# A hybrid recurrence and feed-forward layer: activations turned in 32x32 blocks by VectorE and placed by DRAM transfers, with silu(z) multiplied in the output stage

## The chip, the cores and the metric

The kernel runs on one core of a Trainium2 chip. The metric is the device time of one execution in microseconds, here the median of three runs. Inputs and outputs lie in DRAM; five engines (PE for matmuls, DVE, ACT, POOL, and SP, which only issues transfers) run their own instruction streams and wait for each other through semaphores.

## The reference, cut to what matters

One layer is computed for 2048 rows of one new stream and for 8 running streams of 16 rows, 17 tiles of 128 rows in all. Everything is float32.

```
h   = RMSNorm_pre(x);  P = h @ w_in -> q, k, v, z (512 each), b, a (4), B, C, H (512 each)
q, k, v: causal conv(4), SiLU, q and k L2-normalised; gated delta rule over chunks -> o (4 heads x 128)
o   = RMSNorm_head(o; gdn_norm_w) * silu(z)
y   = B * causal_conv3(C * H)
x   = x + RMSNorm_post(concat(o, y) @ w_o)
h   = RMSNorm_pre2(x)                       # norm_ffn_pre
x   = x + RMSNorm_post2((silu(h @ w_gate) * (h @ w_up)) @ w_down)
```

D_MODEL is 1024, D_FF 2816. The states and the last rows before the convolutions are outputs too.

## The kernel before, in words

Each float32 operand of a large matmul is split into a high and a low part, and a product is three matmuls (high x high, high x low, low x high), accumulated in PSUM. Rows of a tile lie on the 128 partitions or, turned, features lie on them; a matmul contracts over the partitions, so an activation has to be turned so that its features are there.

The program has four stages. (1) 0 to 860 us: the in-projection and the recurrence, in five groups of tiles (`GROUPS = [[0..3], [4..7], [8, 9, 10], [11, 12, 16], [13, 14, 15]]`; tile 16 is the sample rows). PE's order here is written out by hand: actions of the recurrence are put at slots between the in-projection's matmuls. `out_norm` scales a tile's output o (rows on partitions, 4 heads x 128 features) by its norm; `out_turn` (L717) turns the four 128x128 blocks on PE (L720) into a PSUM bank, multiplies on DVE by the gain `g_hd` and by silu(z) (L722), which already lies with features on partitions, and stores the tile `ot` to the DRAM tensor `mixo[t]` on ACT's queue. The other half of the mixture goes to `mixs` per group. (2) 860 to about 1065 us: the output stage. `o_load(t)` loads `mr` from `mixo[t]` (L1095, 128 rows of 2 KB) and `mixs` (L1097) and the residual row tile `xo` (L1099), all on SP's queue. `o_tile(t)` splits `mr` into `mh` and `ml` (L1068 on ACT, L1069 on DVE), runs 48 matmuls of 512 columns against the split `w_o` (L1116, into `dbank` and `tbank`), squares the sums (L1120, ACT), takes the root on POOL (`rstd`, L147), multiplies by `gpost` (L1125, DVE) and adds the residual (L1126). `o_rows(t)` makes the feed-forward input: squares (L1135, ACT), root (L147, POOL), `hx` = row scaled (L1139, DVE), eight PE transposes into two PSUM banks `ftbank` (L1145), two DVE multiplications by the gain `g_ffn` into `ht` (L1146), and a store of `ht` to `hTd` on ACT's queue (L1149). There is one `mr` buffer and three `mh`/`ml` pairs of half a tile. While tiles 7 to 13 are in this stage the first feed-forward group is prepared: `ffn_load` (L1236) loads `fh` from `hTd` for the six tiles of the group, one load of 128 rows of 3 KB for each of the 8 blocks of 128 features, and `ffn_prep` forms sums and splits of them. (3) 1090 to 1985 us: gate and up products (L1351) for the groups of tiles 0 to 5, 6 to 11 and 12 to 16, in a Strassen-like form; the weights are combined and split on ACT, DVE and POOL (L1326, L1327), stored once to `fsplit` and loaded again for later groups. The `fh` of groups 1 and 2 are loaded in this stage (L1236, 8 loads each). (4) to 2457 us: the down product (L1528) and the final norm.

Apart from PE's hand-written slots in stage 1, each engine's order and the order of SP's queue are set when the program is built, by a scheduler that simulates it with its own costs. On the chip each queue then runs in exactly that order: SP issues transfers one after the other, and an instruction whose wait is not fulfilled holds up all behind it on its engine.

## Time and profile before

| | before |
|---|---|
| runs (us) | 2456.3, 2461.07, 2460.23; median 2460.23 |
| profiled execution: span, first to last instruction (us) | 2457.2 |
| time of the profiled execution outside its span | not given separately; the three runs lie 0.9 below to 3.9 above its span |
| PE busy | 2428.1 us, 99% |
| DVE, ACT, POOL busy | 1619.9, 1045.7, 578.6 us |
| DMA, mean rate | 228 GB/s |

PE is busy nearly throughout, so its idle time and its instructions make up the span. A matmul is pipelined: its listed duration runs past the start of the next one, and what an instruction costs PE is read from the distance between starts.

### The profile page before, as it was taken

How to read it: one execution, taken by the hardware profiler on the slowest of the kernel's cores; microseconds unless marked ns; L12 is line 12 of the kernel's file. 1: busy time of each engine (PE TensorE's matmuls, PEld its weight loads, DVE VectorE, ACT ScalarE, POOL GpSimd, SP SyncE). 2: the span in 40 equal slices, each digit the busy share in tenths (PEclk: the TensorE clock that was granted, in tenths of full speed). 3: DMA queues.
4: the chain of work that ended last, by engine and by line, in shares of the span. 5: the costliest groups of instructions: out<-in, count | busy, mean ns of one | idle time of the engine just before them, and what ended most of it. 6: DMA issues, size and time to landing. Idle time of an engine off the chain costs nothing.

```text
span 2457.2 us, 39354 instructions
## 1 busy us (share of the span) xinstructions
PE 2428.1 (99%) x14376; PEld 2222.2 (90%) x14376; DVE 1619.9 (66%) x3079; ACT 1045.7 (43%) x2338; POOL 578.6 (24%) x664
## 2 busy tenths in 40 slices
PE   9999999999999999999999999999999999999997
PEld 7888889999989978899999999999999988887886
DVE  7875755746667366788888644556555565677698
ACT  6545546546444343444444422324333345333343
POOL 1101001001110000156655200000000046455563
PEclk9999999999999999999999999999999999999999
DMA  7774655666776466598877788778898743333465
GB/s 272 262 246 163 220 194 203 244 222 232 273 261 234 162 222 225 195 336 301 289 268 259 266 261 266 252 246 273 307 298 283 249 144 118 116 111 122 132 224 191
DMA packets 263465, 561.38 MB, mean 228 GB/s; under 512 B 25188, under 2 KB 144680, under 8 KB 245992
## 3 DMA queue, kind: packets, MB, share of 16 engines
q1 hardware_dynamic: 146864, 486.98, 57.3%
q10 hardware_dynamic: 116184, 70.85, 9.5%
q8 instruction: 113, 1.85, 0.3%
q0 software_dynamic: 224, 1.05, 0.1%
q14 instruction: 80, 0.66, 0.1%
HBM read 400.09 MB, written 158.70 MB: 227 GB/s over the span
## 4 chain that ended last, share of the span: by engine, by line
PE 87%; DVE 6%; DMA 2%; issue 2%; POOL 2%; ACT 1%; SPq 0%; DVEq 0%; ACTq 0%; POOLq 0%
PE fbank L1351 36%; PE dbank L317 26%; PE fbank L1528 11%; PE dbank L1116 4%; PE tbank L1116 4%; POOL dw L1201 1%; DVE xr L1551 1%; PE tbank L375 1%; DVE acc L1488 1%; PE gbank L592 1%; PE gbank L599 1%; PE obank L769 1%; POOL as L1511 1%; PE obank L747 1%; PE gbank L739 1%
## 5 line engine op out<-in xcount | busy, mean ns | idle before, releaser
L1351 PE MATMUL fbank<-xh,fw 128*128 128x384 f32 (+1 forms) x3696 | 898.1, 326 | 2.7 <-ACT m L1385 2.5
L317 PE MATMUL dbank<-hi,w 128*128 128x384 f32 (+1 forms) x2240 | 655.6, 363 | 2.2 <-DMA w<-wsplit 1.4
L1351 PEld LDWEIGHTS fbank<-xh,fw 128*128 128x128 f32 x3696 | 651.6, 188 | 3.4 <-ACT m L1385 2.8
L1351 PE MATMUL fbank<-xl,fw 128*128 128x384 f32 (+1 forms) x1848 | 602.4, 326 | 0.0
L317 PEld LDWEIGHTS dbank<-hi,w 128*128 128x128 f32 x2240 | 412.6, 188 | 43.9 <-issue 4.0
L1528 PE MATMUL fbank<-dw,as 128*128 128x512 f32 x1782 | 420.2, 392 | 3.4 <-DVE as L1511 1.2
L1528 PEld LDWEIGHTS fbank<-dw,as 128*128 128x128 f32 x1782 | 332.9, 188 | 82.1 <-POOL as L1511 3.5
L317 PE MATMUL dbank<-lo,w 128*128 128x384 f32 (+1 forms) x1120 | 399.6, 357 | 0.3 <-DVE lo L232 0.3
L1351 PEld LDWEIGHTS fbank<-xl,fw 128*128 128x128 f32 x1848 | 347.3, 188 | 0.0
L317 PEld LDWEIGHTS dbank<-lo,w 128*128 128x128 f32 x1120 | 210.7, 188 | 16.6 <-DVE lo L232 0.6
L1511 POOL TENSOR_TENSOR as<-ar,as 128x256 fp32r<-128x256 f32 (+1 forms) x202 | 184.2, 924 | 171.1 <-ACT as L1508 168.7
L1488 DVE TENSOR_TENSOR acc<-acc,fbank 128x512 f32<-128x512 f32 x248 | 164.9, 681 | 90.2 <-PE fbank L1528 77.1
L1201 POOL TENSOR_TENSOR dw<-dr,dw 128x512 fp32r<-128x512 f32 x48 | 70.3, 1477 | 497.5 <-ACT dw L1199 497.3
L1508 ACT CAST as<-ar 128x256 fp32r<-128x256 f32 (+1 forms) x287 | 116.4, 427 | 166.8 <-PE fbank L1528 124.3
L1326 ACT CAST fw<-rg 128x512 fp32r<-128x512 f32 x124 | 77.2, 622 | 228.6 <-PE fbank L1351 138.3
L321 DVE SCALAR_TENSOR_TENSOR acc<-R,vec,acc 128x512 f32<-128x512 f32 (+2 forms) x180 | 120.9, 672 | 27.0 <-ACT acc L358 20.8
L1399 DVE TENSOR_TENSOR c<-u,fbank 128x384 f32<-128x384 f32 (+1 forms) x66 | 34.8, 528 | 95.5 <-PE fbank L1351 95.5
L1395 DVE TENSOR_TENSOR m<-m,m 128x384 f32<-128x384 f32 (+1 forms) x44 | 23.1, 525 | 82.8 <-ACT m L1385 82.8
L1327 POOL TENSOR_TENSOR fw<-rg,fw 128x512 fp32r<-128x512 f32 x44 | 65.3, 1485 | 45.9 <-ACT fw L1326 41.9
L1397 ACT ACTIVATE m<-fbank 128x384 f32<-128x384 f32 (+1 forms) x66 | 31.2, 473 | 96.4 <-PE fbank L1351 79.0
L350 POOL COPY hist<-R 128x3 f32<-128x3 f32 x60 | 20.1, 335 | 220.6 <-ACT R L326 171.5
L1402 ACT ACTIVATE c<-c 128x384 f32<-128x384 f32 (+1 forms) x66 | 33.4, 507 | 83.4 <-DVE c L1401 83.4
(395 smaller groups left out, 3575.6 us busy)
## 6 DMA issues: line engine op xcount, KB each, us to landing
w<-wsplit SPq DMA_DIRECT2D x105, 1024.0 KB, 4.9
fw<-fsplit SPq DMA_DIRECT2D x188, 512.0 KB, 4.8
fsplit<-fw SPq DMA_DIRECT2D x94, 512.0 KB, 3.6
partd<-pt ACTq DMA_DIRECT2D x86, 384.0 KB, 6.1
rg<-in_w_gu SPq DMA_DIRECT2D x62, 512.0 KB, 4.0
wsplit<-w SPq DMA_DIRECT2D x28, 1024.0 KB, 4.9
wr<-in_w_in SPq DMA_DIRECT2D x34, 512.0 KB, 5.8
ar<-partd SPq DMA_DIRECT2D x43, 384.0 KB, 3.1
```

The lines of the kernel that those rows point to most:

```text
L317: T.matmul(ps[:, :c], l[:, k, :], r[k][:, :c], start=(k == 0 and r is hi and l is wh), stop=(k == KD - 1 and l is wl))
L321: r = V.scalar_tensor_tensor(acc, raw(d), w[:, d:d + 1], acc, op0=ALU.mult, op1=ALU.add)
L1116: T.matmul(pss[n], m_[:, j, :], w_[k][:, n * 512:(n + 1) * 512], start=(k == 0 and ci == 0), stop=(k == KD - 1 and ci == 2))
L1201: e.tensor_tensor(out=w[1], in0=v, in1=w[0].bitcast(F32), op=ALU.subtract)
L1326: A.copy(w[:, 0], v)
L1327: e.tensor_tensor(out=w[:, 1], in0=v, in1=w[:, 0].bitcast(F32), op=ALU.subtract)
L1351: T.matmul(ps, w_[:, c], b_[k][:, :hw], start=(first and k == 0 and ci == 0), stop=(k == KH - 1 and ci == 2), skip_group_check=not first)
L1399: V.tensor_add(c21, u2, b3)
L1488: return eng.tensor_tensor(out=dst, in0=dst, in1=ps, op=ALU.add)
L1508: ins = A.copy(a[:, 0, :n], v)
L1511: e.tensor_tensor(out=a[:, 1, :n], in0=v, in1=a[:, 0, :n].bitcast(F32), op=ALU.subtract)
L1528: T.matmul(ps, a[:, x_, q * P:(q + 1) * P], w[y_], start=(start and q == 0 and ci == 0), stop=(q == c - 1 and ci == 2), skip_group_check=True)
```

## The change: turning moved to VectorE and to transfers

Both places that turned activations on PE now turn them on DVE in 32x32 blocks (an instruction that exchanges rows and columns inside each 32x32 block of a tile), and the blocks get to their places by the way in which the tile is stored to DRAM and loaded again.

- Recurrence output: `out_turn` is one DVE instruction, `V.transpose(ot, o)`. `mixo[t]` is now [4 heads, 4, 32*128], written in rows of 512 B (512 of them), and read by `o_load` in rows of 128 B (2048 of them). Features within a head come out in the order `turn` (a 4x32 index array turned), which the host applies to z's columns of `w_in`, to `gdn_norm_w` and to the first four blocks of rows of `w_o`.
- silu(z) and the gain: silu(z) of a group is stored to a new DRAM tensor `szd[gi]` on ACT's queue when its fourth head is done; `o_load` loads the tile's part `zr` (512 rows of 512 B) on SP's queue, and POOL multiplies the tile's `mr` by it, 128x512 (for tile 0, in `ahead`, eight loads and four POOL multiplications of 128x128). The gain `g_hd` goes into the split of `w_o`: for its first four blocks the ACT copy has a scale and the DVE subtraction becomes a scalar_tensor_tensor.
- Feed-forward rows: in `o_rows` the scaling and the gain are one DVE instruction for each half of 512 features, into a PSUM tile now called `hx`, followed by one DVE 32x32 transpose of the half into `ht`. The gain is a broadcast row tile `gffn` (128x1024), loaded on SP's queue behind `gpost`. `ht` is stored with 1024 rows of 512 B as before. `fh` is loaded in 3072 rows of 128 B (2560 in the group of five tiles) in place of 128 rows of 3 KB (2.5 KB). The features within a block of 128 come out in the order `turn`, which the host applies to the rows of the gate and up weights.

The diff, cut to its core (indices into the small vector table shift and are left out):

```
-    mixo = [dram.tile([P, H, P], F32, name=f"mixo{t}") for t in range(NT)]
+    mixo = [dram.tile([H, 4, 32 * P], F32, name=f"mixo{t}") for t in range(NT)]
+    szd = [dram.tile([P, H, len(g) * P], F32, name=f"szd{gi}") for gi, g in enumerate(GROUPS)]
...
-    hTd = [dram.tile([P, KD, len(g) * P], F32, name=f"hTd{gi}") for gi, g in enumerate(FGROUPS)]
+    hTd = [dram.tile([KD, 4 * len(g), 32 * P], F32, name=f"hTd{gi}") for gi, g in enumerate(FGROUPS)]
...
                 flush(mark["A"])
+                if h == 3:
+                    nc.scalar.dma_start(out=szd[g["gi"]], in_=g["sz"][:, :, :c])
...
         def out_turn(g, i, o):
-            ps = tbank()
-            for h in range(H):
-                T.transpose(ps[:, h * P:(h + 1) * P], o[:, h, :], ident)
             ot = wk.tile([P, H, P], F32, tag="ot", name="ot")
-            V.scalar_tensor_tensor(ot, h4(ps), g_hd, g["sz"][:, :, i * P:(i + 1) * P], op0=ALU.mult, op1=ALU.mult)
+            V.transpose(ot, o)
+            out = mixo[g["tiles"][i]].rearrange("h a (d x) -> (a d) h x", d=32)
             if i + 1 < g["npr"] or g["gi"] + 1 < len(GROUPS):
-                nc.scalar.dma_start(out=mixo[g["tiles"][i]], in_=ot)
+                nc.scalar.dma_start(out=out, in_=ot)
             else:
-                last_stores.append((mixo[g["tiles"][i]], ot))
+                last_stores.append((out, ot))
...
-            nc.sync.dma_start(out=vt, in_=mixo[0])
             gi, i = PLACE[0]
+            zs = [q[:, W1 - P:] for q in g["qT"]]
+            for h in range(H):
+                nc.sync.dma_start(out=vt[:, h].rearrange("p (a t) -> p a t", a=4), in_=mixo[0][h].rearrange("a (p t) -> p a t", t=32))
+                nc.sync.dma_start(out=zs[h], in_=szd[gi][:, h, i * P:(i + 1) * P])
             nc.sync.dma_start(out=sz, in_=mixs[gi][:, :, i * P:(i + 1) * P])
+            for h in range(H):
+                G.tensor_tensor(out=vt[:, h], in0=vt[:, h], in1=zs[h], op=ALU.mult)
...
+        def wo_split(k, a, b, v):
+            if k < H:
+                A.activation(a, v, AF.Copy, scale=g_hd)
+                V.scalar_tensor_tensor(b, v, g_hd, a.bitcast(F32), op0=ALU.mult, op1=ALU.subtract)
+            else:
+                A.copy(a, v)
+                V.tensor_sub(b, v, a.bitcast(F32))
...
         nc.sync.dma_start(out=gpost, in_=rows_[0].partition_broadcast(P))
+        nc.sync.dma_start(out=gffn, in_=rows_[2].partition_broadcast(P))
...
-                m = oa.tile([P, KD, P], F32, tag="mr", name="mr") if t > 1 else spare[2]
+                m = oa.tile([P, KD, P], F32, tag="mr", name="mr") if t > 1 else spare[1]
                 mr = m[:, 0:4], m[:, 4:8]
-                nc.sync.dma_start(out=mr[0], in_=mixo[t])
                 gi, i = PLACE[t]
+                zr = oa.tile([P, 4, P], F32, tag="zr", name="zr")
+                nc.sync.dma_start(out=mr[0].rearrange("p h (a t) -> p (h a) t", a=4), in_=mixo[t].rearrange("h a (p t) -> p (h a) t", t=32))
+                nc.sync.dma_start(out=zr, in_=szd[gi][:, :, i * P:(i + 1) * P])
                 nc.sync.dma_start(out=mr[1], in_=mixs[gi][:, :, i * P:(i + 1) * P])
+                G.tensor_tensor(out=mr[0], in0=mr[0], in1=zr, op=ALU.mult)
...
-            hx = op.tile([P, D], F32, tag="hx", name="hx") if t else spare[0]
-            V.tensor_scalar_mul(hx, xt, r)
-            ht = op.tile([P, KD, P], F32, tag="ht", name="ht") if t else spare[1]
+            ht = op.tile([P, D], F32, tag="ht", name="ht") if t else spare[0]
             for n in range(2):
-                ps = pft.tile([P, 512], F32, tag="t", name="ftbank")
-                for q in range(4):
-                    k = 4 * n + q
-                    T.transpose(ps[:, q * P:(q + 1) * P], hx[:, k * P:(k + 1) * P], ident)
-                V.tensor_mul(ht[:, 4 * n:4 * n + 4, :], ps.rearrange("p (k c) -> p k c", k=4),
-                             g_ffn[:, 4 * n:4 * n + 4].unsqueeze(2).broadcast_to([P, 4, P]))
+                c = slice(n * 512, (n + 1) * 512)
+                hx = pft.tile([P, 512], F32, tag="t", name="hx")
+                V.scalar_tensor_tensor(hx, xt[:, c], r, gffn[:, c], op0=ALU.mult, op1=ALU.mult)
+                V.transpose(ht[:, c], hx)
             gi, i = FPLACE[t]
-            nc.scalar.dma_start(out=hTd[gi][:, :, i * P:(i + 1) * P], in_=ht)
+            nc.scalar.dma_start(out=hTd[gi][:, 4 * i:4 * i + 4].rearrange("k a (d x) -> (a d) k x", d=32),
+                                in_=ht.rearrange("p (k x) -> p k x", k=KD))
...
-                nc.sync.dma_start(out=h[:, :2 * hw], in_=hTd[gi][:, k, :])
+                nc.sync.dma_start(out=h[:, :2 * hw].rearrange("p (m t) -> p m t", t=32), in_=hTd[gi][k].rearrange("m (p t) -> p m t", t=32))
...
+    turn = np.arange(P).reshape(4, 32).T.reshape(P)
...
+    cols = lambda c, b: off[c] + P * b + (turn if c == "z" else np.arange(P))
...
+    a["w_o"] = np.concatenate([w_o[:H, turn], w_o[H:]])
+    a["w_gu"] = gu.reshape(2, KD, P, NF, P)[:, :, turn].transpose(3, 0, 2, 1, 4)
```

The scheduler gives a new order. On SP's queue, at the place in the output stage where the first feed-forward group's `fh` is loaded, `mr_10257` is tile 9's mixture before and `mr_10155` with `zr_10156` after (the tile is the number behind `mixo`); `xo` are residual rows. Before:

```order
L1095 DMA mr_10257<-mixo9_69 128x512
L1097 DMA mr_10257<-mixs2_79 128x4x128
L1236 DMA fh_10118<-hTd0_110 128x768
L1236 DMA fh_10120<-hTd0_110 128x768
L1236 DMA fh_10122<-hTd0_110 128x768
L1236 DMA fh_10124<-hTd0_110 128x768
L1099 DMA xo_10137<-in_x 128x1024
L1236 DMA fh_10225<-hTd0_110 128x768
L1236 DMA fh_10227<-hTd0_110 128x768
L1236 DMA fh_10229<-hTd0_110 128x768
L1236 DMA fh_10231<-hTd0_110 128x768
L1095 DMA mr_10380<-mixo10_70 128x512
```

After, on the same queue at the same place:

```order
L1109 DMA zr_10156<-szd2_79 128x4x128
L1113 DMA xo_9929<-in_x 128x1024
L1247 DMA fh_10021<-hTd0_115 128x24x32
L1247 DMA fh_10023<-hTd0_115 128x24x32
L1247 DMA fh_10025<-hTd0_115 128x24x32
L1247 DMA fh_10027<-hTd0_115 128x24x32
L1247 DMA fh_10123<-hTd0_115 128x24x32
L1247 DMA fh_10125<-hTd0_115 128x24x32
L1247 DMA fh_10127<-hTd0_115 128x24x32
L1247 DMA fh_10129<-hTd0_115 128x24x32
L1108 DMA mr_10155<-mixo9_69 128x16x32
L1110 DMA mr_10155<-mixs2_84 128x4x128
```

Tile 9's mixture stood ahead of the eight `fh` loads and now stands behind all of them; its `zr` is still ahead. On POOL's queue, in the output stage, the rows are the two roots of each tile (`oxr` for the first norm, `oyr` for the second; `oxr_10219` is tile 8's) and, after the change, the multiplications by silu(z) (`mr_10037` is tile 8's mixture, `mr_10155` tile 9's, `mr_10273` tile 10's). After:

```order
L1111 TENSOR_TENSOR mr_10037<-mr_10037,zr_10038 128x512
L147 TENSOR_TENSOR oxr_9987<-oxm_9985,neghalf_181 128x1
L147 TENSOR_TENSOR oyr_9999<-oym_9997,neghalf_181 128x1
L147 TENSOR_TENSOR oxr_10101<-oxm_10099,neghalf_181 128x1
L147 TENSOR_TENSOR oyr_10113<-oym_10111,neghalf_181 128x1
L147 TENSOR_TENSOR oxr_10219<-oxm_10217,neghalf_181 128x1
L1111 TENSOR_TENSOR mr_10155<-mr_10155,zr_10156 128x512
L147 TENSOR_TENSOR oyr_10231<-oym_10229,neghalf_181 128x1
L1111 TENSOR_TENSOR mr_10273<-mr_10273,zr_10274 128x512
```

Before, only the alternating `oxr` and `oyr` rows stood there; now tile 9's multiplication stands behind `oxr_10219`, and each root behind a multiplication waits for that tile's loads.

## Rows read from the trace of the kernel before

**Rows 1.** The page: busy time of each engine, and the chain that ended last.
```profile
PE 2428.1 (99%) x14376; PEld 2222.2 (90%) x14376; DVE 1619.9 (66%) x3079; ACT 1045.7 (43%) x2338; POOL 578.6 (24%) x664
...
PE 87%; DVE 6%; DMA 2%; issue 2%; POOL 2%; ACT 1%; SPq 0%; DVEq 0%; ACTq 0%; POOLq 0%
```

**Rows 2.** Waits of PE: releaser, us in total, times, longest.
```profile
PE fbank L1351 <- ACT m L1385: 2.5, 1, 2.5
```

**Rows 3.** Groups of PE instructions: count, busy us, mean ns, idle before.
```profile
L1145 PE MATMUL ftbank<-cst,hx 128*128 128x128 f32 x136 | 17.7, 273 | 0.2 <-DVE hx L1139 0.2
L720 PE MATMUL tbank<-cst,o 128*128 128x128 f32 x64 | 9.7, 274 | 0.0
```

**Rows 4.** Timeline of PE around eight transposes: start, duration, instruction.
```profile
946.91 0.40 PE L1116 MATMUL tbank<-wol,mh 128*128 128x512 f32 x1
947.14 1.04 PE L1145 MATMUL ftbank<-cst,hx 128*128 128x128 f32 x8
947.93 0.47 PE L1116 MATMUL dbank<-woh,ml 128*128 128x512 f32 x1
948.25 0.39 PE L1116 MATMUL tbank<-woh,ml 128*128 128x512 f32 x1
```

**Rows 5.** Timeline of PE at tile 1's second half.
```profile
869.36 0.50 PE L1116 MATMUL dbank<-woh,mh 128*128 128x512 f32 x1 [0.49 <-ACT mh L1068]
```

**Rows 6.** Timeline of ACT and its queue in the output stage.
```profile
868.69 0.62 ACT L1068 CAST mh<-mr 128x512 fp32r<-128x512 f32 x1 [3.84 <-DMA mr<-mixo]
...
933.54 0.59 ACT L1120 ACTIVATE ojunk<-dbank 128x512 bf16<-128x512 f32 x1
...
950.89 0.52 ACTq L1149 DMA_DIRECT2D hTd<-ht  x1
...
957.47 0.62 ACT L1068 CAST mh<-mr 128x512 fp32r<-128x512 f32 x1 [3.97 <-DMA mr<-mixo]
```

**Rows 7.** Timeline of POOL after tile 5's matmuls.
```profile
935.47 0.55 POOL L147 TENSOR_TENSOR oxr<-oxm,neghalf 128x1 f32<-128x1 f32 x1 [5.03 <-DVE oxm L145]
```

**Rows 8.** Timeline of SP's queue at tile 9's loads.
```profile
952.87 0.33 SPq L1095 DMA_DIRECT2D mr<-mixo  x1
...
954.41 2.34 SPq L1236 DMA_DIRECT2D fh<-hTd  x4
...
957.27 2.29 SPq L1236 DMA_DIRECT2D fh<-hTd  x4
```

**Rows 9.** Transfers at 857.3 to 858.8: packets, MB, share of 16 engines.
```profile
q10 hardware_dynamic: 144, 0.00, 5.1%
...
out_sc_p<-shist ACTq DMA_DIRECT2D x1, 4.0 KB
```

**Rows 10.** Transfers at 793.0 to 794.0, the store of conv_p (144-B rows).
```profile
q10 hardware_dynamic: 117, 0.02, 9.8%
```

**Rows 11.** Transfers at 938.9 to 941.2, 512-B rows of hTd and x2d stores.
```profile
q10 hardware_dynamic: 730, 0.37, 50.4%
```

**Rows 12.** Groups of DVE and POOL instructions by form.
```profile
L1146 DVE TENSOR_TENSOR ht<-ftbank,vec 128x512 f32<-128x512 f32 x34 | 22.2, 682 | 7.6 <-PE ftbank L1145 7.6
...
L1125 DVE SCALAR_TENSOR_TENSOR dbank<-dbank,oxr,gpost 128x512 f32<-128x512 f32 x17 | 12.9, 758 | 10.6 <-POOL oxr L147 10.6
...
L633 DVE STREAM_TRANSPOSE utd<-Ts 128x512 f32<-128x512 f32 x5 | 5.8, 1163 | 0.2
...
L786 POOL TENSOR_TENSOR AU<-kt,tl 128x512 f32<-128x512 f32 x1 | 1.0, 1037 | 0.0
...
L1327 POOL TENSOR_TENSOR fw<-rg,fw 128x512 fp32r<-128x512 f32 x44 | 65.3, 1485 | 45.9 <-ACT fw L1326 41.9 <-PE fbank L1351 4.0
```

**Rows 13.** Stretches: us; PE, PEld, DVE, ACT, POOL busy; PEclk, DMA share, GB/s.
```profile
1160.00:1200.00 40.00, 40.00 (x233) 40.00 (x232) 30.75 (x37) 15.24 (x31) 23.89 (x18) 1.00 0.87 297
1360.00:1400.00 40.00, 37.51 (x214) 37.12 (x213) 25.91 (x51) 19.37 (x45) 11.27 (x6) 0.98 0.86 298
1400.00:1440.00 40.00, 40.00 (x227) 40.00 (x226) 20.45 (x37) 11.41 (x22) 0.00 (x0) 0.97 0.77 241
```

More of the change, by code (lines that the diff above doesn't have):

```diff
@@ L133 @@
     ident, ones = cst[:, 0:128], cst[:, 128:256]
-    vec = const.tile([P, 147], F32, name="vec")
+    vec = const.tile([P, 139], F32, name="vec")
     nc.scalar.dma_start(out=vec, in_=vecs)
@@ L1056 @@
         pft = ps_p.enter_context(tc.tile_pool(name="pft", bufs=3, space=PSUM, reuse_waits="tile"))
-        gpost = op.tile([P, D], F32, name="gpost")
+        gpost, gffn = (op.tile([P, D], F32, name=nm) for nm in ("gpost", "gffn"))
         ojunk = op.tile([P, 512], BF16, name="ojunk")
-        spare = [op.tile([P, D], F32, tag="hx", name="hx"), op.tile([P, KD, P], F32, tag="ht", name="ht"),
-                 oa.tile([P, KD, P], F32, tag="mr", name="mr")]
+        spare = [op.tile([P, D], F32, tag="ht", name="ht"), oa.tile([P, KD, P], F32, tag="mr", name="mr")]
         wo = {k: [oa.tile([P, D], F32R, name=f"{nm}{k}") for nm in ("woh", "wol")] for k in reversed(range(KD))}
@@ L1076 @@
                     a, b = (h4(w[:, 512 * q:512 * q + 512]) for w in (wh, wl))
-                    A.copy(a, v)
-                    V.tensor_sub(b, v, a.bitcast(F32))
+                    wo_split(k, a, b, v)
             else:
@@ L1081 @@
                 nc.sync.dma_start(out=wr, in_=w_o[k])
-                A.copy(wh, wr)
-                V.tensor_sub(wl, wr, wh.bitcast(F32))
+                wo_split(k, wh, wl, wr)
             if k < 2:
@@ L1686, in pack @@
     a["state"] = f["state_gdn"][0]
[L1687 to L1688 removed]
+    a["vecs"] = np.concatenate([f["norm_mix_pre"][0].reshape(KD, P).T,
+                                f["gdn_norm_w"][0][turn].reshape(1, P).T, conv_w.reshape(P, 48), sc_w.reshape(P, 12),
                                 w_ba.reshape(P, 64), gates], axis=1)
[L1690 removed]
+    a["rows"] = np.concatenate([f["norm_mix_post"], f["norm_ffn_post"], f["norm_ffn_pre"]])
     a["consts"] = shape_constants()
```

21 lines of the change are left out of this document (8 added, 13 removed).

## The prediction

> **What bounds the kernel now.** I read the page first. PE is busy 99% of the span and makes 87% of the chain that ended last [rows 1]; the other engines have room. So only two things change the time: PE instructions that go, and times at which PE waits. The list of PE's waits comes next: the longest of the whole program is 2.5 us [rows 2], so every load, cast and root is hidden today, and the question is which of them comes late after the change. Third are the groups by form, for the instructions that leave PE and those that come to DVE and POOL [rows 3, 12]; fourth the timelines of PE, ACT, POOL and SP's queue in the output stage, where the change adds work between DRAM and matmul [rows 4 to 8]; last the DMA views of three short stretches, which give the price of a packet by its size [rows 9 to 11].
>
> **PE transposes go.** 136 of them leave the feed-forward rows and 64 and four more of another tile the recurrence [rows 3]. Their listed durations overlap the neighbours. In the timeline two matmul starts lie 0.23 us apart; with eight transposes between, the stretch from 946.91 to 948.25 holds two matmul steps and the transposes, so they cost 1.34 - 2 x 0.23 = 0.88 us [rows 4]. 17 tiles x 0.88 = 15.0. The recurrence's groups of four cost half, 0.44, and 16 of the 17 count (behind the last one PE waits for a cast anyway): 7.0. Sum -22.0 us; from 947.14 to 947.93 alone it would be 0.79 and -19.8, by the listed busy times 17.7 + 9.7 = -27.4. A tile of the output stage then takes 48 x 0.226 = 10.85 us.
>
> **Start of the output stage: +4.6.** Tile 1's first cast already starts when its load lands, at 868.69 [rows 6], and PE waits 0.49 us for it at 869.36 [rows 5]. So this chain has no room. It now gets: the gain row `gffn`, 512 KB, ahead of it in SP's queue (at 297 GB/s of [rows 13] 1.8 us); the 128-B load of `mixo`; `zr`; and POOL's multiplication. For packets the trace shows 8.5 ns each for rows of 32 B (1.5 us x 16 engines x 5.1% / 144, [rows 9]), 13.4 ns for rows of 144 B (1.0 x 16 x 9.8% / 117, [rows 10]) and 25.4 ns for rows of 512 B (2.3 x 16 x 50.4% / 730, [rows 11]). A load of 128-B rows is not in the trace; the nearest row is the 144-B one, so I take 13.4 ns, with 8.5 and 25.4 as ends. Then `mixo` takes 2048 x 13.4 / 16 = 1.7 us in place of 0.9 (256 KB at 297 GB/s), and `zr` 512 x 25.4 / 16 = 0.8. POOL's multiplication of 128x512 is bounded by 1.04 and 1.49 us [rows 12]; I take 1.25. 1.8 + 0.8 + 0.8 + 1.25 = 4.6; from 2 (where only POOL and `zr` are not overlapped) to 6.5 (25.4 ns and 1.49).
>
> **Tile 9: +16.4.** This is the largest new wait. In SP's queue the eight `fh` loads of group 0 now stand ahead of tile 9's mixture, which stood ahead of them before. They need tile 5's `hTd` store, and each is 3072 packets of 128 B: 3072 x 13.4 / 16 = 2.6 us, eight 20.6. I count from the end of tile 5's matmuls (933.54, where ACT starts to square its sums, [rows 6]). Before, that tile's store was issued 17.4 us later, at 950.89 [rows 6], and the loads 3.5 us behind it, at 954.41 [rows 8]. The transposes stood at 947.14, 13.6 us after the end [rows 4]; in their place come two scalings (0.76 each) and two 32x32 transposes (up to 1.16 each, [rows 12]) on DVE, which no longer wait for a slot on PE, and the scaling before goes: the store comes at about +15.5, the loads at +19. The train ends at +39.6; in its time ACT's queue stores at least two further `x2d` and `hTd` pieces of 1024 packets of 512 B, 1.6 us each on all engines: +43. Behind it the mixture's 1.7, some 2 us to land, POOL's 1.25 and the cast's 0.62 ([rows 6]) give +48.9. PE is due at tile 9 after tiles 6, 7 and 8, 3 x 10.85 = 32.5. So PE stands for 16.4 us; what is queued behind it is PE's whole order, and nothing fills it. With 8.5 ns the train takes 13.0 and the wait is 8.9 us; with 25.4 ns 39 and 35 us. From below POOL's order gives a bound that no transfer lifts: tile 9's multiplication stands behind the root of tile 8, which ended 2.5 us after a tile's end (935.47 + 0.55 against 933.54, [rows 6, 7]); plus 1.25 and 0.62 PE waits at least 4.4.
>
> The Trainium skill speaks to the packet's price from two sides. The page "DMA: Bandwidth & Descriptors", section "Why small descriptors are slow (HBM only)", counts about three cycles for each packet on top of one for 32 bytes; as an estimate that is 7 cycles for 128 B and 19 for 512 B, so 7/19 of 25.4 = 9.4 ns, a train of 14.4 us, a wait of 10 and a sum of some -4. The section "Specifications" of the same page wants 512 B for full rate and says that below it the engine reads, modifies and writes; by that a 128-B row would cost no less than a 512-B one. The trace lies between: 144 B took 13.4 ns, about half of a 512-B row, but on a store.
>
> **Clock: +2.5.** After the 2.5-us wait in 1360 to 1400 the granted clock is 0.98 there and 0.97 in the next 40 us though PE is busy throughout [rows 13]: 0.8 + 1.2 = 2.0 us given away. Two waits come, so 0 to 4; I take 2.5.
>
> **Feed-forward stage: +1.** Groups 1 and 2 load `fh` in 128-B rows too: 8 loads x (2.6 - 1.3) and 8 x (2.1 - 1.1) = 18 us of all engines, over 600 us in which weight loads are ahead of their use; the engines' share is 0.87 where it is high [rows 13]. Hidden, at 1 us; if the loads get in the way of the weights, all 18.
>
> **At nothing.** DVE gets per tile 2 x 0.76 + 2 x 1.16 at most and loses 2 x 0.68 and a scaling [rows 12]; it is busy 26 of 40 us and less around it [rows 13] and this lies one tile ahead of PE. POOL's other multiplications take 1.25 of a 10.85-us tile, and POOL is busy 24% [rows 1]. The stores of silu(z) are on ACT's queue in a stage with DMA room; the gain in `w_o`'s split costs a scale that ACT's copy carries and a DVE form of near the same length. If this cover goes, each tile gives one multiplication, 17 x 1.25 = 21 us.
>
> **Sum.** -22.0 + 4.6 + 16.4 + 2.5 + 1 = +2.5 us on the profiled execution of 2457.2, that is 2459.7. The median of the runs stands 3.0 above that span, and the change is the same against it: 2462.7, rounded 2463. This kernel's runs tell 0.2%, 4.9 us, from no change, so this is no measurable change.
>
> **Rivals.**
> A. *Small packets are cheap.* At 8.5 ns a packet and with the train less disturbed by the stores, tile 9 waits 6.5 us, the start costs 3.5, the clock 1.5: -22 + 3.5 + 6.5 + 1.5 + 0.5 = -10, 2450. The 32-B row speaks for it [rows 9]; against it that a 144-B row took more [rows 10]. With POOL's bound alone, 4.4, a start of 2 and no loss of clock it would be 2445. The skill's page on descriptors, cited above, lies between this and the forecast.
> B. *A 128-B row costs as much as a 512-B row* (slower): a train of 39 us, a wait of 35 at tile 9, the start 6.5, the clock 3: -22 + 6.5 + 35 + 3 + 1 = +23.5, 2484. It decides from about 15 ns a packet on. For it: no load of such rows is in the trace, and reads from DRAM in short rows may cost more than stores; against: 13.4 ns at 144 B.
> C. *The feed-forward loads are in the way*: weights queue behind sixteen long `fh` loads and PE waits 18 us: +2.5 + 17 = 2480. For it: the DMA share 0.87; against: the longest wait of PE anywhere is 2.5 us today [rows 2], so the loads are made well ahead.
>
> **How the numbers follow.** The forecast has 0.45, with a range of its own of 2457 to 2470 (13.4 ns give or take 2 moves the wait by 3, the start by 2, the clock by 2); A 0.27, B 0.18, C 0.10. The range of 8 in 10 takes in most of A and B: 2446 to 2483. Faster by over 0.2%: all of A and 0.03 of the forecast, 0.30. Slower: B, C and 0.11 of the forecast's upper part, 0.39. The rest, 0.31, is within 0.2%.
>
> **What would show it.** In the profile after: PE's groups without transposes and tiles of the output stage 10.85 us apart; a wait of PE for `mh` near tile 1 of 2 to 7 us; one of 9 to 20 at tile 9, with `mh` released by POOL's product and that by the mixture's load, which is issued right behind the `fh` loads but lands after them; `fh` landing times that grow along the train by 2.6 us each; the granted clock below 1.00 after both waits. I am wrong if the `fh` train ends before +30 (then A), if PE waits in the gate and up stage (C), or if the tiles of the output stage are longer than 11 us apart, since then POOL's product or the short loads limit every tile and not one.

## The result and the profile after

The changed kernel takes 2470.89 us (median of five runs, 2468.58 to 2472.08) against 2460.23 (2456.3 to 2464.33): a ratio of 1.0047, 95% interval 1.0035 to 1.0059. It is slower by some 11 us. Every run of it ends 1.8 us above its own span; the profiled one has a span of 2470.3, 13.1 above the 2457.2 of before.

The page of the changed kernel, answering to [rows 1]: PE has 204 instructions fewer and 13.9 us less work, but its share of the chain that ended last has halved, from 87% to 44%.

```profile
PE 2414.2 (98%) x14172; PEld 2208.3 (89%) x14172; DVE 1637.9 (66%) x3096; ACT 1048.7 (42%) x2338; POOL 601.5 (24%) x684
...
PE 44%; DVE 8%; DMA 3%; issue 3%; POOL 2%; ACT 1%; SPq 0%; ACTq 0%; DVEq 0%; POOLq 0%
```

PE's waits (releaser, us in total, times, longest), answering to [rows 2]; before, the longest was 2.5 us:

```profile
PE dbank L1130 <- ACT mh L1072: 19.7, 3, 16.3
...
PE fbank L1362 <- DVE xo L1140: 2.8, 1, 2.8
PE fbank L1362 <- ACT m L1394: 2.5, 2, 2.3
...
PE tbank L1130 <- DVE xo L1140: 1.3, 2, 1.0
```

One wait of 16.3 us stands out. PE's timeline shows it at the first matmul of tile 9, and behind it matmuls of 512 columns 0.43 us apart in place of 0.23, PE's clock at the lower of its two levels, 1.2 and 2.4 GHz:

```profile
982.10 0.80 PE L1130 MATMUL dbank<-woh,mh 128*128 128x512 f32 x1 [16.31 <-ACT mh L1072]
982.70 0.63 PE L1130 MATMUL tbank<-woh,mh 128*128 128x512 f32 x1
983.12 0.63 PE L1130 MATMUL dbank<-wol,mh 128*128 128x512 f32 x1
983.55 0.63 PE L1130 MATMUL tbank<-wol,mh 128*128 128x512 f32 x1
```

SP's queue at the same place, answering to [rows 8]: the eight `fh` loads take 19.7 us to be issued, where before two lots of four took 2.3 each, and tile 9's `mr` comes behind them.

```profile
955.22 19.72 SPq L1247 DMA_DIRECT2D fh<-hTd  x8
975.04 1.94 SPq L1108 DMA_DIRECT2D mr<-mixo  x1
977.02 1.17 SPq L1110 DMA_DIRECT2D mr<-mixs  x1
```

POOL and ACT meanwhile (answering to [rows 6, 7]). Tile 8's root ran at 974.06, late, since ACT's own queue had stood: its store of `ht` and the square behind it waited 9.6 us for an `fh` transfer to end. The product of tile 9 then waited 5.5 us more, for the mixture's load, so that it is the load, and not ACT's stand, that set its time here.

```profile
974.06 0.55 POOL L147 TENSOR_TENSOR oxr<-oxm,neghalf 128x1 f32<-128x1 f32 x1 [2.79 <-DVE oxm L145]
980.13 1.26 POOL L1111 TENSOR_TENSOR mr<-mr,zr 128x512 f32<-128x512 f32 x1 [5.53 <-DMA mr<-mixo]
```
```profile
966.48 0.38 ACTq L1159 DMA_DIRECT2D hTd<-ht  x1
966.98 0.63 ACT L1149 ACTIVATE ojunk<-xo 128x512 bf16<-128x512 f32 x1 [9.62 <-DMA fh<-hTd]
...
971.41 0.59 ACT L1134 ACTIVATE ojunk<-dbank 128x512 bf16<-128x512 f32 x1
...
981.43 1.14 ACT L1072 CAST mh<-mr 128x512 fp32r<-128x512 f32 x2 [8.62 <-POOL mr L1111]
```

The transfers of 960 to 968 us are almost only the 128-B rows (packets, MB, share of 16 engines), answering to [rows 9 to 11]. Reckoned as the prediction did there, with the share, a packet took 8 x 16 x 120.4% / 11,946 = 12.9 ns. The share is above 100%, since packets overlap on an engine; on each engine one began every 8 x 16 / 11,946 = 10.7 ns.

```profile
q1 hardware_dynamic: 11946, 1.52, 120.4%
```

Three stretches of the changed kernel (us; PE, PEld, DVE, ACT, POOL busy; PEclk, DMA share, GB/s), answering to [rows 13]: the granted clock falls at the start of the output stage and after tile 9's wait. Before, it was 1.00 in both 10-us stretches shown first.

```profile
860.00:870.00 10.00, 5.88 (x17) 3.68 (x15) 3.28 (x4) 2.83 (x4) 1.26 (x1) 0.83 1.04 313
870.00:880.00 10.00, 9.86 (x36) 7.99 (x37) 4.66 (x5) 4.27 (x6) 1.34 (x1) 0.83 0.88 264
...
982.00:992.00 10.00, 9.90 (x34) 8.03 (x35) 8.89 (x17) 3.65 (x10) 1.80 (x2) 0.76 0.81 238
```

The new instructions, answering to [rows 12]: the scaling into PSUM 0.81 us, the 32x32 transposes 0.69, POOL's product 1.31.

```profile
L1156 DVE SCALAR_TENSOR_TENSOR hx<-xo,oyr,gffn 128x512 f32<-128x512 f32 x34 | 26.2, 814 | 8.4 <-POOL oyr L147 8.4
L1157 DVE STREAM_TRANSPOSE ht<-hx 128x512 f32<-128x512 f32 x34 | 22.4, 690 | 0.0
```
```profile
L1111 POOL TENSOR_TENSOR mr<-mr,zr 128x512 f32<-128x512 f32 x16 | 21.0, 1314 | 65.8 <-DMA mr<-mixo 36.5 <-DMA zr<-szd 14.0 <-DVE oym L145 10.0
```

**Where the 13.1 us are.** The starts, in PE's timeline, of the first matmul of the output stage, of the gate and up stage and of the down stage cut each profiled execution into four parts (us). A single execution can stand some us from its kernel's median (e2's is 2459.5 + 1.8 against 2466.2), so the table tells where time lies, and the medians tell how much.

| kernel | recurrence, until | output stage | gate and up | down | span |
|---|---|---|---|---|---|
| before | 860.9 | 202.0 | 918.6 | 475.7 | 2457.2 |
| after | 857.2 | 217.7 | 919.5 | 475.8 | 2470.3 |
| e1_mix_only | 853.4 | 212.0 | 925.4 | 475.1 | 2465.9 |
| e2_rows_only | 859.9 | 207.4 | 917.2 | 475.0 | 2459.5 |
| e3_split | 855.7 | 213.7 | 918.2 | 475.9 | 2463.5 |
| e4_big_rows | 856.4 | 212.3 | 918.8 | 476.2 | 2463.6 |
| e5_rows_spread | 860.2 | 195.7 | 931.1 | 476.1 | 2463.1 |
| e6_all_spread | 855.1 | 207.6 | 918.6 | 475.3 | 2456.6 |
| e7_spread_no_silu | 856.1 | 197.3 | 920.4 | 476.8 | 2450.7 |
| e8_rows_spread_late | 861.5 | 194.1 | 929.6 | 476.2 | 2461.3 |
| e9_rows_spread2 | 860.9 | 197.5 | 919.9 | 476.1 | 2454.4 |
| e10_all_dve | 856.4 | 209.7 | 917.5 | 476.2 | 2459.8 |
| e11_light_dve | 862.4 | 189.8 | 926.2 | 475.8 | 2454.1 |
| e12_pool_rows | 861.4 | 190.0 | 931.6 | 476.4 | 2459.4 |

The recurrence ends 3.7 us earlier, the output stage is 15.7 longer, the rest 1.0. In the output stage 816 matmuls at 0.2265 us make 184.8 in both kernels. Of the 17.2 us beyond that before, 14.1 were transposes (15 groups of eight; a tile takes 11.81 us with one and 10.88 without; two more groups stood in the next stage), 1.3 waits, 1.8 the rest. Of the 32.9 after, 24.7 are waits (16.3 at tile 9; 4.3 at the start; 1.3 for `xo` at two tiles; 2.8 at the first gate and up matmul) and 8.2 are matmuls further apart than 0.2265: the lower clock at the two places above. The sum, after less before: recurrence -3.7, transposes -14.1, tile 9 +16.3, start +2.9, `xo` +1.3, change of stages +2.8, clock and the rest 8.2 - 1.8 = +6.4, later stages +1.0; together 12.9 of the 13.1.

### The profile page after: what moved, and what is told of

It is laid out like the page before. It is cut to its first block, busy times and chain, and to the rows that moved or that the text cites. A ratio compares the mean times of both kernels' runs of the same rounds, so it can differ in the third digit from the quotient of the medians.

```text
span 2470.3 us, 39058 instructions
## 1 busy us (share of the span) xinstructions
PE 2414.2 (98%) x14172; PEld 2208.3 (89%) x14172; DVE 1637.9 (66%) x3096; ACT 1048.7 (42%) x2338; POOL 601.5 (24%) x684
## 3 DMA queue, kind: packets, MB, share of 16 engines
q0 software_dynamic: 224, 1.05, 0.1%
## 4 chain that ended last, share of the span: by engine, by line
PE 44%; DVE 8%; DMA 3%; issue 3%; POOL 2%; ACT 1%; SPq 0%; ACTq 0%; DVEq 0%; POOLq 0%
PE fbank L1362 35%; PE fbank L1539 10%; POOL dw L1212 1%; DMA mr<-mixo 1%; DVE acc L1499 1%; DVE xr L1562 1%; DMA dr<-in_w_dn 1%; POOL as L1522 1%; DVE acc L1557 0%; DVE fw L1338 0%; DVE as L1522 0%; DVE hx L1156 0%; POOL mr L1111 0%; DMA ar<-partd 0%; DVE xo L1140 0%
## 5 line engine op out<-in xcount | busy, mean ns | idle before, releaser
L1130 PE MATMUL dbank<-woh,mh 128*128 128x512 f32 x136 | 54.4, 400 | 20.9 <-ACT mh L1072 19.7
```

The costliest lines, as they stand in the source:

```text
L1130: T.matmul(pss[n], m_[:, j, :], w_[k][:, n * 512:(n + 1) * 512], start=(k == 0 and ci == 0), stop=(k == KD - 1 and ci == 2))
```

## The experiments

All times are medians against the kernel before on the same chip, whose medians there were 2456.9 to 2457.8; the ratio, with its 95% interval, is not the quotient of the medians and lies up to 0.001 from it. Differences between two experiments are told only where their intervals do not overlap, or as unsettled.

**e1_mix_only.** The recurrence half of the change alone; `o_rows`, `hTd` and the `fh` loads are those of before.

```
-                V.scalar_tensor_tensor(hx, xt[:, c], r, gffn[:, c], op0=ALU.mult, op1=ALU.mult)
-                V.transpose(ht[:, c], hx)
+                    T.transpose(ps[:, q * P:(q + 1) * P], hx[:, k * P:(k + 1) * P], ident)
+                V.tensor_mul(ht[:, 4 * n:4 * n + 4, :], ps.rearrange(...), g_ffn...)
```

> Only the recurrence half of the change (out_turn on VectorE, mixo in 128-B rows, silu(z) stored, loaded and multiplied by POOL, the gain in w_o); the feed-forward rows are turned on PE as before and fh is loaded in 3-KB rows. The queue theory (tile 9's mixture behind eight loads of short rows in SP's queue makes the loss): SP's order has tile 9's mixture ahead of fh again, so no wait of more than 4 us for mh at tile 9; minus 7 for the transposes, plus about 3 us lost in the recurrence and 3 at tile 1: 2457 to 2463. Rival (POOL's multiplication and its place between the roots, and the 128-B load of each mixture, cost PE in every tile or at tile 9): PE waits for mh at tile 9 or at several tiles, 2470 or more.

Measured: 2469.43, 1.0046 (1.0029 to 1.0063). The wait at tile 9 is gone, as the queue theory says (its order has the mixture ahead of `fh`), but the time is not what it gave: this half alone loses as much as the whole. Its recurrence ends 7.5 us earlier, all of the 7 expected; the output stage then loses 10 and the next stage 6.8. PE's waits in it:

```profile
PE dbank L1131 <- ACT mh L1074: 3.7, 2, 2.7
PE fbank L1366 <- ACT m L1398: 3.0, 3, 1.7
PE fbank L1366 <- ACT m L1400: 2.5, 1, 2.5
PE ftbank L1160 <- DVE hx L1154: 2.3, 2, 1.8
PE ftbank L1160 <- DVE oss L1136: 2.0, 3, 0.8
```

No wait is long. Many are short, at the start (2.7, and 1.9 for the split of `w_o`), through the tiles, and where the gate and up stage begins; the 2.5 for ACT is the one of before [rows 2]. The rival's sign, a wait at tile 9 or waits for `mh` at several tiles, is missing too. So the queue's order is one cause, not the only one; and the halves are not additive, since this one alone costs as much as both together.

**e2_rows_only.** The feed-forward half alone, on the kernel before (PE turns in `out_turn`, no `zr`, no product on POOL).

```
-                T.transpose(ps[:, q * P:(q + 1) * P], hx[:, k * P:(k + 1) * P], ident)
+                V.scalar_tensor_tensor(hx, xt[:, c], r, gffn[:, c], op0=ALU.mult, op1=ALU.mult)
+                V.transpose(ht[:, c], hx)
...
-                nc.sync.dma_start(out=h[:, :2 * hw], in_=hTd[gi][:, k, :])
+                nc.sync.dma_start(out=h[:, :2 * hw].rearrange("p (m t) -> p m t", t=32), in_=hTd[gi][k].rearrange(...))
```

> Only the feed-forward half (rows scaled, gained and turned on VectorE, hTd stored in blocks, fh loaded in 128-B rows); the recurrence turns on PE as before, with 2-KB mixture rows, no zr and no POOL multiplication. In SP's order tile 9's mixture again stands behind the eight fh loads. The queue theory: the long wait stays, 13 to 16 us at tile 9 (the POOL product's 1.3 us is gone); minus 15 for the transposes, plus 15, plus 2 to 3 for the clock and some 3 us at the start of the gate and up stage: 2462 to 2468. Rival (POOL's multiplication, standing behind the root of tile 8, holds tile 9): the wait shrinks to a few us and the time falls to 2447 to 2452.

Measured: 2466.20, 1.0032 (1.0020 to 1.0043), within the theory's 2462 to 2468. The wait at tile 9 is there without POOL's product, 15.2 us, again behind eight `fh` loads in SP's queue:

```profile
978.36 0.80 PE L1116 MATMUL dbank<-woh,mh 128*128 128x512 f32 x1 [15.20 <-ACT mh L1067]
```
```profile
949.72 22.52 SPq L1233 DMA_DIRECT2D fh<-hTd  x8
972.34 2.39 SPq L1095 DMA_DIRECT2D mr<-mixo  x1
```

The rival with POOL's product as cause falls. Its mixture is loaded in 2-KB rows, so the short rows of `mixo` are not the cause either.

**e3_split.** The whole change, with the last four `fh` loads issued behind tile 9's mixture.

```
-            hs += hload
             prep = ffn_prep(0, hs, fs=fs)
...
+                if i == 0:
+                    with tc.issue_after(omark["S"].ins):
+                        hs += hload
```

> The whole change, but the last four fh loads of group 0 are issued behind tile 9's mixture; it stands behind four and not eight. The queue theory: tile 9's mixture lands 8 to 10 us earlier, the wait falls from 16.3 to 5 to 8 us, the clock falls less: 2458 to 2463. If only the first-come place in SP's queue counted and four loads fitted in the time PE has, 2455. Rival (ACT's queue, in which tile 8's squares stood until 971.4 behind stores that waited for fh transfers to end, and with them tile 8's root ahead of POOL's product): the wait stays at 11 us or more and the time at 2466 or more.

Measured: 2465.35, 1.0029 (1.0019 to 1.0040): above the theory's 2458 to 2463, and with an interval that overlaps the changed kernel's. The wait at tile 9 fell to 6.8 as the theory gave, but the next tile, now behind the other four loads, waits 3.3 and 2.2:

```profile
969.52 0.80 PE L1132 MATMUL dbank<-woh,mh 128*128 128x512 f32 x1 [6.79 <-ACT mh L1072]
...
986.25 0.50 PE L1132 MATMUL dbank<-woh,mh 128*128 128x512 f32 x1 [3.25 <-ACT mh L1072]
```

The rival, that ACT's held queue would keep the wait at tile 9 at 11 us or more, falls. But part of a long train's cost passes from one tile to the next: the three waits make 12.2 of the 16.3, and in this execution the wait at tile 1 was 4.1 in place of 2.4.

**e4_big_rows.** SP's order kept by hand, `fh` read in rows of 3 KB. The blocks are not put in their places, so the feed-forward input is permuted.

```
-                nc.sync.dma_start(out=h[:, :2 * hw].rearrange("p (m t) -> p m t", t=32), in_=hTd[gi][k].rearrange(...))
+                omark["F"] = nc.sync.dma_start(out=h[:, :2 * hw], in_=hTd[gi][:, k, :])
...
+                with tc.issue_after(omark["F"].ins) if t == 9 else ExitStack():
```

> The whole change with SP's order kept (tile 9's mixture behind all eight fh loads), but hTd laid out so that fh is read in 128 rows of 3 KB; the turned blocks are then not put in their places, so the feed-forward input is permuted wrongly. Packet theory: the train takes some 9 to 11 us in place of 20, the wait at tile 9 falls to 5 to 8 us; groups 1 and 2 change nothing: 2457 to 2463. Rival (only the order and the wait for tile 5's store count, the packet size does not): the wait stays at 14 us or more and the time within 3 us of the changed kernel's 2471. Second rival (short rows of groups 1 and 2 also cost in the gate and up stage): the time falls by more than the wait does, to 2450.

Measured: 2466.00, 1.0032 (1.0021 to 1.0043). The train is issued in 4.0 us in place of 19.7, but the wait at tile 9 falls only to 10.4, more than the 5 to 8 expected, and the time misses its range too; the rest of SP's queue then stands at the next load, 7.3 us:

```profile
956.64 4.01 SPq L1249 DMA_DIRECT2D fh<-hTd  x8
...
961.29 0.37 SPq L1111 DMA_DIRECT2D mr<-mixo  x1
962.29 7.33 SPq L1113 DMA_DIRECT2D mr<-mixs  x1
```
```profile
975.57 0.79 PE L1133 MATMUL dbank<-woh,mh 128*128 128x512 f32 x1 [10.41 <-ACT mh L1072]
```

So of 16.3 us long rows in `fh` take away about 6. About 10 stay; they hold the place behind 3 MB that wait for tile 5's store, and also the mixture's own short rows, which e4 keeps. The gate and up stage did not change (918.8 against 919.5): the short rows of groups 1 and 2 are hidden there, as forecast.

**e5_rows_spread and e8_rows_spread_late.** The feed-forward half with the preparation of group 0 one tile later (`O_SPLIT = 8`) and four `fh` loads behind tile 9's mixture, four behind tile 10's; e8 also loads `gffn` behind tile 1's residual rows.

```
-O_SPLIT = 7
+O_SPLIT = 8
...
+            with tc.issue_after(omark["S"].ins):
+                hs = [next(hload) for _ in range(KH)]
```

> The feed-forward half alone, as in the earlier run of that half, but the preparation of group 0 is moved one tile later and its fh loads go out four behind tile 9's mixture and four behind tile 10's, so each mixture stands behind at most four loads that need not be there in time for it. Theory (the place of the mixtures in SP's queue makes the 15-us wait): no wait of more than 3 us for mh, the clock stays at 1.00 past 880, and with minus 15 for the transposes and plus 2 at tile 1: 2445 to 2451, faster than before. Rival (the number of short-row packets keeps the transfers engines or the queues' completion slots busy whatever the order, and the wait moves to tile 10 or 11 or to the start of the gate and up stage): waits of 8 us or more in sum remain, 2455 or more.

> The feed-forward half with spread loads, and the gain row gffn is loaded behind the residual rows of tile 1 and not ahead of tile 1's mixture. If its 512 KB in front of the mixture make the 2.5-us wait at tile 1 of the half alone, that wait falls back to about 0.5 us as before the change, and the time is 2 us below the same kernel with the early load: 2443 to 2449. Rival (it comes in time anyway and the wait is the packets' own): no difference.

Measured: 2464.90, 1.0024 (1.0013 to 1.0034), and 2462.56, 1.0014 (1.0003 to 1.0025). Both theories missed, and e5's rival had its outcome, waits at the start of the next stage and 2455 or more. The output stage did what the theory gave: 195.7 and 194.1 us, 6 to 8 under before, with one wait of 4.1 left. But the gate and up stage grew to 931.1 and 929.6, by 11 to 12 us, most of it in waits for ACT and VectorE at its start (e5):

```profile
PE dbank L1118 <- ACT mh L1067: 6.2, 3, 4.1
PE fbank L1353 <- ACT m L1385: 3.5, 1, 3.5
PE fbank L1353 <- DVE ht L1145: 2.7, 1, 2.7
PE fbank L1353 <- ACT m L1386: 2.3, 2, 1.2
```

In e8 the wait at tile 1, 1.8 us in e5, is gone: the gain row ahead of tile 1's mixture made it. In time the two runs' intervals overlap.

**e6_all_spread and e7_spread_no_silu.** The whole change with the same spreading, and the same without `zr` and product for tiles 1 to 16 (their output lacks silu(z)).

```
-                zr = oa.tile([P, 4, P], F32, tag="zr", name="zr")
-                nc.sync.dma_start(out=zr, in_=szd[gi][:, :, i * P:(i + 1) * P])
-                G.tensor_tensor(out=mr[0], in0=mr[0], in1=zr, op=ALU.mult)
```

> The whole change with the same spreading of the fh loads (four behind tile 9's mixture, four behind tile 10's). Theory: the 16.3-us wait and some 2.5 us of clock go, what is left are the losses at the start of the output stage (about 3 us of waits and 3 us of clock), in the recurrence and at the start of the gate and up stage: 2449 to 2456. Rival (POOL's product between the roots and the short-row mixture loads hold tiles 9 to 11 as well): waits for mh of 6 us or more remain in that stretch, 2458 to 2465.

> As the whole change with spread loads, but silu(z) is not multiplied for tiles 1 to 16 (neither the zr loads nor POOL's products; the output lacks the factor). If the zr load and POOL's product are what makes tile 1 late at the start, the wait for mh there falls from 2.4 to under 1 us, the clock stays up, and the time is 4 to 6 us below the run with the product. Rival (the gain row's load ahead of it and the w_o split with its scale make the start late): the wait stays above 2 us and the time is within 2 us of the run with the product.

Measured: 2461.25, 1.0011 (1.0002 to 1.0021), and 2450.75, 0.9966 (0.9954 to 0.9977). With the order (and the preparation one tile later) the change comes to 0.0011 above before, some 3 us, where the changed kernel stood at 0.0047, with intervals apart. But the time lies in the rival's range, 2458 to 2465, and not in the theory's: the wait at tile 9 is gone, and waits for `mh` of 3.3 and 1.8 came at tiles 10 and 11, less than the rival's 6. Without the `zr` loads and the product it is 10.5 us faster still, more than the 4 to 6 expected and the first version clearly faster than before. The wait at tile 1 falls from 2.4 to 0.4, and PE's clock stays up earlier: 0.74 and 0.91 with the product, against 0.83 and 1.00 in the same two stretches without (e7):

```profile
860.00:870.00 10.00, 7.90 (x26) 5.59 (x27) 4.52 (x5) 4.68 (x6) 0.00 (x0) 0.83 0.99 308
870.00:880.00 10.00, 10.00 (x46) 8.26 (x45) 4.97 (x5) 3.59 (x4) 0.00 (x0) 1.00 0.73 196
```

In the profiled executions the output stage shows it: 197.3 against 207.6, of which waits 3.5 and matmuls further apart than 0.2265 us 6.8.

**e10_all_dve.** The whole change, loads spread, gain row late, preparation placed as in e9, product on VectorE.

```
-                G.tensor_tensor(out=mr[0], in0=mr[0], in1=zr, op=ALU.mult)
+                V.tensor_tensor(out=mr[0], in0=mr[0], in1=zr, op=ALU.mult)
```

> The whole change, fh loads spread and the preparation placed as in the other run of this call, the gain row late, and the product with silu(z) on VectorE in place of POOL. The version without the product stood 10 us below the one with it. Theory 1 (POOL's 1.26 us and its place in POOL's queue between the roots make the price): most of it comes back, 2447 to 2453. Theory 2 (the zr loads ahead of the mixtures, each waiting for a completion slot in SP's queue, make the price): nothing comes back, 2457 to 2464, with waits for mh at tile 1 of 2 us or more.

Measured: 2464.52, 1.0022 (1.0011 to 1.0032). Nothing came back. But e10 differs from e6 in three things, and VectorE, now with the product ahead of its other work, made PE wait 3.3 us for `xo`; so it shows only that the product on VectorE is no better, not that POOL's duration costs nothing. That the `zr` loads are the price is not shown either: theory 2 asked for 2 us or more at tile 1, and with the gain row late there were 0.6. What of the 10 us is the loads, POOL's duration, or the product's place in the chain from load to cast stays open.

**e9_rows_spread2, e11_light_dve, e12_pool_rows.** The feed-forward half, spread, with the preparation ending at the tile where it ended before (e9); the same with tiles 14 to 16 only scaled by ACT, so that their feed-forward input lacks the gain and the turn (e11); and complete, with ACT and POOL scaling tiles 13 to 16 and VectorE only turning (e12).

```
+            o_tile(O_SPLIT + 1)
...
+                if t >= 14:
+                    A.activation(ht[:, c], xt[:, c], AF.Copy, scale=r)
+                    continue
...
+                if t >= 13:
+                    A.activation(hx, xt[:, c], AF.Copy, scale=r)
+                    G.tensor_tensor(out=hx, in0=hx, in1=gffn[:, c], op=ALU.mult)
```

> The feed-forward half alone, fh loads spread as before (four behind tile 9's mixture, four behind tile 10's), the gain row late, but the last parts of group 0's preparation are put back to the tiles where they stood before the change (two parts beside tile 10). Theory: what the earlier spread version lost again at the start of the gate and up stage (12 us) came from the preparation that ended a tile later and kept the first weights' buffers; then the gate and up stage takes 918 to 922 us again and the whole 2446 to 2453. Rival (VectorE and the first weights' casts set the start of that stage, so whatever is gained ahead of it is given back): the stage takes 926 us or more and the time stays within 4 us of 2463.

> The last feed-forward-half version (loads spread, preparation back in place), but tiles 14 to 16 are only scaled, by ACT, and neither multiplied by the gain nor turned, so their feed-forward input is wrong: VectorE is relieved of 2.9 us for each of them just where the gate and up stage begins, and they take no PSUM bank for hx. If VectorE's queue at the change of stages gives the gains back, the two waits of 3.9 us there (for the last tiles' xo and ht on VectorE) fall to 2 us or less in sum and the time to 2450 to 2454. If not VectorE but the arrival of the first weights holds PE there, the time stays within 2 us of 2459.8.

> The same version, complete in its result: for tiles 13 to 16 ACT scales the rows and POOL multiplies by the gain, in SBUF and not in a PSUM bank, and VectorE only turns; that takes 1.5 us for each of these tiles from VectorE. If VectorE's queue at the change of stages is what holds PE, 2453 to 2457, about half of what the run without any of this work gains; if POOL's two products of 1.3 us, ahead of the first weights' products in its queue, take its place, 2459 or more.

Measured: e9 2459.75, 1.0008 (0.9999 to 1.0017); e11 2451.84, 0.9972 (0.9962 to 0.9981); e12 2458.36, 0.9997 (0.9984 to 1.0009). In e9 the gate and up stage is back at 919.9, as its theory gave, but PE now waits at the change of stages, twice 3.9 us, for VectorE's work on the last tiles, so the time only equals before. It is not the 2446 to 2453 of the theory but within the 4 us of 2463 that its rival gave, though not by a longer stage:

```profile
1058.38 0.41 PE L1356 MATMUL fbank<-xh,fw 128*128 128x384 f32 x1 [3.89 <-DVE xo L1130]
...
1068.25 0.44 PE L1356 MATMUL fbank<-xh,fw 128*128 128x384 f32 x1 [3.91 <-DVE ht L1147]
```

The first of these waits falls on a busy VectorE (8.64 of the 10 us from 1050 on), the second does not: VectorE itself stood idle for 4.43 us there, until a store of `ht` had landed. There is one `ht` buffer, and this store took 12.5 us to land, where the median in the output stage is 4.4, so that the next tile's transposes and all behind them in VectorE's order had to wait (the store's issue with its size and time to landing, then VectorE):

```profile
hTd<-ht ACTq DMA_DIRECT2D x1, 512.0 KB, 12.5
```
```profile
1067.48 1.31 DVE L1147 STREAM_TRANSPOSE ht<-hx 128x512 f32<-128x512 f32 x2 [4.43 <-DMA hTd<-ht]
```

Taking the row work of three tiles from VectorE (e11) gives 8 us in the medians (0.0036 in the ratios), as its expectation said, and these two waits are gone. Its profiled execution (span 2454.1, the slowest of its runs) has one wait of 3.6 for ACT later, with a lower clock behind it. e12, which moves half of the work, is no different from e9 and missed both of its ranges. Its profile shows where the gain goes: its output stage is 12.0 us shorter than before, and its gate and up stage 13.0 longer. VectorE stood again for the `ht` store, 4.92 us, though it had less to do and the scaled rows took no PSUM bank, and PE waited for what stood behind it:

```profile
1075.46 0.71 DVE L1152 STREAM_TRANSPOSE ht<-hs 128x512 f32<-128x512 f32 x1 [4.92 <-DMA hTd<-ht]
...
1077.41 1.01 PE L1361 MATMUL fbank<-xh,fw 128*128 128x384 f32 x2 [3.37 <-DVE fw L1337]
```

So the gains are given back at this place through VectorE's order; how much of that is VectorE's time and how much the one `ht` buffer with its slow store is not separated, since e11 takes both away. A version with a second `ht` buffer was not run. No complete version beat the kernel before beyond its interval.

## Why the prediction was right and where it was wrong

The time lies inside the range (2446 to 2483) and the slower side had the largest chance, 0.39, though the predicted value, 2463, said no measurable change. Against before the measured 11 us stand beside a sum of 2.5. Against the profile's 13.1, the terms that were too low are the clock (by 3.9), the recurrence's transposes (3.3), the change of stages (2.8, put at nothing) and the wait for `xo` at two tiles (1.3); only the start was too high (1.7).

**Tile 9: the mechanism right, the exact number luck.** 16.4 forecast, 16.3 measured, by the mechanism named: e2 shows the wait without POOL, e3 and e6 that it falls with the order, e4 that long rows take away 6 of the 16. But steps were off and cancelled. Counted from the end of tile 5's matmuls (931.73 in PE's timeline; ACT squared its sums only 2.5 us later), the loads were issued at +23.5 and not +19, since the store came at +19.3 (950.99) and not +15.5; the train was through at +43.3, as forecast (+43), because it took 19.7 us where 20.6 and 3.4 for the stores had been put down; the mixture landed 5.0 us after its issue and not 3.7; and PE was due at +34.1 and not +32.5. The forecast's own terms behind the +43 add up to +48.6, not +48.9. The price of a packet was near: 12.9 ns against 13.4. The condition for rival A (a train that ends before +30) was not met; e4 also shows that even long rows would have left 10.4.

By the Trainium skill, "DMA: Bandwidth & Descriptors", section "Why small descriptors are slow (HBM only)", a 128-B packet was estimated at 9.4 ns; the trace, reckoned like the 25.4 ns that the estimate starts from, gives 12.9, more than that. The section "Specifications" of that page sets 512 B as the least transfer at full rate; if a short row had cost as much as a 512-B one, 25.4 ns [rows 11], rival B would have come, and the trace doesn't agree with that reading.

**Transposes, near in size, partly lost on the way.** A group cost 0.93 us in the output stage (11.81 less 10.88), 0.88 forecast, and that stage lost its 14.1 us of them. The recurrence's 7.0 arrived as 3.7 in the changed kernel's profile and as 7.5 in e1's. These two are the ends of a spread: the seven profiles with the recurrence of before end it at 859.9 to 862.4, 861.0 in the mean, the seven with the changed one at 853.4 to 857.2, 855.8 in the mean, so about 5 of the 7 arrive. In the changed kernel's profile the granted clock was 0.91 at 680 to 700 us, against 1.00 before and in e1, which makes up to 1.8 us; the rest of what was lost stays open.

**Clock, the term that was most mis-sized.** 2.5 us were put down for two waits. The runs give 6.4 in the output stage, with what could not be told apart from it: 2.3 behind tile 9, where ten matmuls start 0.43 to 0.60 us apart before the spacing falls back, and 3.1 at the start, beyond before, where the clock is 0.83 in two stretches of 10 us. The forecast took the price of one wait of 2.5 us from the stage after it; at the start waits of 1.24, 0.58 and 2.44 us come close together, and the clock fell more than behind one: 0.83 over 20 us, against 0.98 and 0.97 over 40 each.

**Start, 4.6 forecast, 2.9 of waits measured**, before the clock. The terms were not additive: the feed-forward half alone, with the gain row, waits 2.5 at tile 1, the other half alone, without it, 2.7, both together 2.4. In the split of `w_o` waits of 1.24 and 0.58 came, where before 0.47 and 0.38 stood. The scale, put at nothing, is not their main reason: a scaled copy takes 1.15 us in place of 1.05. ACT stood 2.1 us for the load of a block of `w_o`, which was issued 0.5 us before the stage began and 2.1 us before it in the kernel before:

```profile
861.04 2.40 ACT L1078 ACTIVATE woh<-wor,vec 128x1024 fp32r<-128x1024 f32 x2 [2.10 <-DMA wor<-in_w_o]
```

**VectorE "at nothing", wrong.** DVE's cover was read in the middle of the gate and up stage [rows 13]. At its start there is none: before the change DVE is busy 19.86 of the 20 us from 1080 on, with the last tiles' rows and the first weights' sums together (a stretch of the kernel before, columns as above):

```profile
1080.00:1100.00 20.00, 19.58 (x115) 19.16 (x115) 19.86 (x25) 8.67 (x16) 13.30 (x9) 1.00 1.02 393
```

The changed kernel waits 2.8 us there, and the versions that came earlier to this place gave back 8 to 12: e5 and e8 in a longer stage, e9 in the two waits. VectorE's time is not all of it: in e9 and e12 VectorE stood idle for the store of `ht`, 4.43 and 4.92 us, a wait that the forecast does not have. It also means that the 22 us of transposes were never all to be had: time gained ahead of this place is partly lost at it.

**Product of silu(z), mis-sized.** It was costed at 1.25 us at tile 1 and 1.25 at tile 9, and its `zr` load at 0.8; e7 against e6 puts both, in all tiles, at 10.

**Gate and up stage, right by luck.** +1 was forecast and +0.9 measured, and rival C did not come: e4 reads all `fh` in long rows and has the same stage. But two larger amounts cancelled. PE did wait in this stage, 1.25 and 2.33 us for ACT and not for weights, and by the 600th of its 5544 matmuls the changed kernel had lost 5.2 us there against before. Later 4.2 came back, since the wait of 2.5 us of the kernel before [rows 2], with its loss of clock, did not come again: in the same stretch PE now is busy throughout, at 1.00.

```profile
1133.17 0.45 PE L1362 MATMUL fbank<-xh,fw 128*128 128x384 f32 x1 [2.33 <-ACT m L1394]
```
```profile
1360.00:1400.00 40.00, 40.00 (x232) 40.00 (x232) 31.93 (x46) 19.76 (x44) 20.67 (x14) 1.00 0.84 301
```

## What to carry to other kernels

When a change makes a transfer's rows shorter, look first at what stands behind it in the same issue queue, and count from the event that the transfer waits for; that found the place and the size of the largest wait here, though the last digit was luck. An engine's room has to be read at the change of stages and not as a mean, since time gained ahead of a place where another engine is full is given back there; and a buffer that only a store's landing frees has to be counted with that engine. And several short waits of PE close together cost more than their sum, in the clock that follows.
